# Feed forward of a two-layer diffusion step: gate and up products by a seven-product scheme, all products up before all products down

## The chip, the cores and the metric

The kernel runs on one core of a Trainium2 chip. The metric is the device time of one execution in microseconds (us), as the median of repeated runs.

## The reference

The model is a backbone of two layers on 1024 latent tokens and 128 context tokens, with 1024 features. Each layer has a token mixer (differential attention in layer 0, windowed attention with a sink in layer 1) and a dense SwiGLU feed forward with 2816 inner columns; RMSNorm stands before and behind both, and a modulation computed from a condition gives shift, scale and gate.

```python
def swiglu(h, w_gate, w_up, w_down):
    return (jax.nn.silu(h @ w_gate) * (h @ w_up)) @ w_down

# per layer, for context (p) and latent tokens (s):
hs = pre_norm_modulate(xs, norm_g[i, 2], ms[3], ms[4])
xs = post_norm_residual(xs, swiglu(hs, w_gate[i], w_up[i], w_down[i]), norm_g[i, 3], ms[5])
```

All of it is in float32. The kernel splits each operand of a large product into a high and a low half that TensorE reads as float32r, and sums three products: high by high, high by low, low by high.

## The kernel before

The 1152 tokens are nine blocks of 128: blocks 0 to 7 are latent, block 8 is the context. The stages follow each other: projections of layer 0, attention, output projection with its norms (class `OProj`), feed forward (class `Ffn`), the same for layer 1. Inside a stage the order of work on TensorE, VectorE, ScalarE and GpSimd is written out by hand (`tc.manual_schedule`): each engine runs its instructions in the order in which the program issues them. The DMA queue is SyncE's alone, and its order is planned by the compiler.

`OProj.step(i)` handles one block: the products of block i (`proj`, two halves), the norms of the block before (`norms`, parts 0 to 2), and the transposition of the block before that (`turn_h`), which leaves its high and low halves in `hT`, in three chunks of three blocks.

`Ffn` goes through the 22 blocks d of 128 inner columns. For each it loads 512 KB of the gate's, the up and the down weights, and splits them (`halves`, `wsplit`: a cast on ScalarE, L96, and a subtraction on VectorE, L97). For each chunk, `half` makes the gate's and the up products (L1327 to L1329: eight blocks kb of features, three products each, 384 columns wide), `swiglu` makes the activations of the block, and `down` multiplies those of the block d before with its down weights (L1353 to L1355, 512 columns) and VectorE adds the sum to `yacc` in SBUF (L1359). So up and down products alternate, and the sums over d are kept in SBUF. The sums of the last two d and the norms behind them follow as a written list of steps (`TAIL`), in layer 0 together with the first projections of layer 1.

Beside the feed forward, `mod_task` computes later parts of the modulation: VectorE accumulates rows of `w_mod` scaled by the condition (L226, L229), the accumulator is split (L96, L97), and four small matmuls (L243) sum over the partitions. It is a generator, and the feed forward takes one step of it per chunk: the split is one step, the matmuls are the next. Layer 0 has six such tasks beside its feed forward, layer 1 one.

PSUM has eight rooms of 512 columns: four `b`, two `t`, two `u`. Transpositions of blocks use `u`.

Of the kernel before, what the change touches and what calls it, by code (L numbers as in the profile page):

```python
# [33 lines left out]
SG = 4  # L34
EPS = 1e-6
LAM_INIT = 0.8 - 0.6 * math.exp(-0.3 * 0)
# [4 lines left out]
def hybrid_step(ctx: ExitStack, tc: tile.TileContext, x_prompt, x_sample, cache_diff_k, cache_diff_v,  # L41
# [14 lines left out]
    # per layer: the six parts of the modulation for both conds, with the norms' gains worked in  # L56
# [4 lines left out]
    # ------------------------------------------------------------------ constants  # L61
# [5 lines left out]
    # column cd of sel[:, cd] is one, the other zero: sums over the partitions into row cd  # L67
# [69 lines left out]
    def pre_norm(rs, xt, G, sh, xn, eng=pool):  # L137
        """xn = xt * rs * G + sh"""
# [3 lines left out]
    def post_norm(yv, rs, gg, xt, xo, t, eng=pool):  # L142
        """xo = xt + gg * yv * rs, the product in t"""
# [6 lines left out]
    def turn_hT(ps, tb, xn, hT):  # L150
        """block tb, transposed and split, into hT"""
        ch, o = tb // 3, (tb % 3) * P
        for half in range(2):
# [4 lines left out]
            hi = hT[0][ch][:, half * 4:half * 4 + 4, o:o + P]  # L158
            lo = hT[1][ch][:, half * 4:half * 4 + 4, o:o + P]
# [8 lines left out]
    class Mod:  # L168
        """parts of the modulation on all partitions, for the cond of the block at hand"""
# [11 lines left out]
    def alloc_hT(pool_, hT=None, chunks=range(3)):  # L181
        """rooms for the transposed input in chunks of three blocks, halves apart"""
        hT = hT or [{}, {}]
        for ch in chunks:
            for f in range(2):
                hT[f][ch] = pool_.tile([P, KB, 3 * P], F32R, name=f"h{'hl'[f]}{ch}")
        return hT
# [13 lines left out]
    def rows_out(l, j, n0, n, r, br, gr):  # L201
        """r: rows of silu(cond) @ w_mod; adds the bias, works in the norm's gain, and keeps them"""
# [11 lines left out]
    def mod_task(sb, ps, l, j, ring):  # L214
        """One of the six 1024-wide parts of the modulation of layer l, for both conds; a generator of steps."""
# [30 lines left out]

    def step(gen, n=1):
# [14 lines left out]
    # ------------------------------------------------------------------ start: conditioning, first modulation  # L262
    class Start:
        """the first modulation, and the first norm block by block"""
# [5 lines left out]
        def modulation(self, hooks):  # L270
            """hooks: by number of the piece of w_mod, what is loaded before it and what follows its split"""
# [45 lines left out]
            # the rows as columns, a feature a partition  # L317
# [19 lines left out]
        def spread(self, j):  # L337
            """the samples' columns as rows on all partitions: a column on all columns times the identity"""
# [35 lines left out]
        def modulate(self, tb):  # L374
            """the gain and the shift of each feature, and the split"""
            ch, o, cd, ts = tb // 3, (tb % 3) * P, cond_of(tb), []
# [10 lines left out]
            for half, t in enumerate(ts):  # L387
                hi, lo = [self.hT[f][ch][:, half * 4:half * 4 + 4, o:o + P] for f in range(2)]
# [11 lines left out]
    def small_params(sb):  # L400
        """lambda, the gain of the norm of the heads, the sinks"""
# [15 lines left out]
    class Ring:  # L417
        """rooms for weights as they come and for their two halves, 4 KiB each, taken in turn"""
# [15 lines left out]

    def ring_rooms(pool_, tags):
        """lays rooms out in the order of their tags"""
# [19 lines left out]
    class Qkv:  # L456
        """columns n * 512.. of the projection of block tb, in steps: products, rope and split, transposes"""

        def __init__(self, l, ps, sb, ring, hT):
            self.l, self.ps, self.sb, self.ring, self.hT = l, ps, sb, ring, hT  # L460
            self.cache = [x[0, 0].rearrange("t h d -> t (h d)") for x in
# [12 lines left out]
        def mm(self, n, tb, k0=0, k1=KB, mid=()):  # L474
            ch, o = tb // 3, (tb % 3) * P
# [3 lines left out]
            for kb in range(k0, k1):  # L479
# [4 lines left out]
                xh, xl = [self.hT[s][ch][:, kb, o:o + P] for s in range(2)]  # L484
# [5 lines left out]
        def split(self, key, x, g, dst, t0, eng=pool):  # L490
            """x[:, 64 g], split, for dst[:, :, t0:t0+128]"""
# [90 lines left out]
        def run(self, order, gens, hooks, g0=0):  # L582
            """hooks: by number of the step, what goes before the products and what goes after them"""
            seq = [(n, tb) for n in order for tb in range(NTB)]
            for i in range(len(seq) + 2):
# [12 lines left out]
                if i < len(seq):  # L598
                    k, tb = i // NTB, seq[i][1]
                    if k + 1 < len(order):  # L600
                        ws = self.ws.setdefault(order[k + 1], [])
                        for k2, (t0, t1) in enumerate(((5, 6), (6, 7), (7, 8), (7, 8))):
                            if tb == t0:
                                ws.append(Wqkv(self.l, self.ring, order[k + 1], k2))
                            if tb == t1:
                                ws[k2].split()
# [1064 lines left out]
```

## Time and profile before

| | |
|---|---|
| median of 3 runs | 3241.43 us |
| lowest and highest run | 3238.78 and 3243.96 us |
| span of the profiled execution, first to last instruction | 3245.7 us |
| instructions | 43729 |
| mean granted clock of TensorE | 0.988 of full speed |
| DMA traffic | 343.87 MB, mean 106 GB/s |

The profile is of one execution on the chip. PE is TensorE's matmuls, PEld its weight loads, DVE is VectorE, ACT ScalarE, POOL GpSimd, SP SyncE, whose queue issues the DMAs. The span of that execution is 4.3 us longer than the median of the runs; no time of its own is listed beside the span.

### The profile page before, as it was taken

What the parts mean: (1) busy time and instruction counts of PE and PEld (TensorE: products, weight loads), DVE (VectorE), ACT (ScalarE), POOL (GpSimd) and SP (SyncE); (2) the same over time, 40 slices, a digit from 0 to 9 for tenths busy, and PEclk for the clock granted to TensorE, in tenths of its full rate; (3) what the DMA queues carried; (4) which work ended last, traced back from release to release, by engine and by line L of the source; (5) the groups of instructions that cost most, each with busy time, mean ns of one, the idle gap of its engine ahead of it and who ended that gap; (6) DMA issues with size and microseconds to landing.
All of it is one profiled execution on the core that took longest, in us unless ns stands there. A gap on an engine that the chain in (4) does not pass through costs nothing. (4 is left out here: it accounts for less than half of the span.)

```text
span 3245.7 us, 43729 instructions
## 1 busy us (share of the span) xinstructions
PE 3107.3 (96%) x16942; PEld 2745.1 (85%) x16942; DVE 2125.8 (65%) x3138; ACT 1081.0 (33%) x2097; POOL 1006.9 (31%) x963
## 2 busy tenths in 40 slices
PE   8999989888999999999999799999999999999997
PEld 5888777777789999999999687777789999999997
DVE  6777388887556666766666944998566544444445
ACT  6332277776551111111112324776431111111112
POOL 2544299999330000000000644666220000000002
PEclk9999999999999999999999899999999999999999
DMA  6665633432442222222223454333442211111113
GB/s 216 205 214 185 204 94 118 130 118 69 140 137 87 76 72 74 82 67 72 85 66 107 163 167 135 111 112 106 138 145 66 65 39 40 46 46 46 39 40 117
DMA packets 309030, 343.87 MB, mean 106 GB/s; under 512 B 13124, under 2 KB 242540, under 8 KB 308696
## 3 DMA queue, kind: packets, MB, share of 16 engines
q1 hardware_dynamic: 308824, 341.09, 33.8%
q8 instruction: 134, 2.20, 0.3%
q14 instruction: 72, 0.59, 0.1%
HBM read 263.62 MB, written 77.41 MB: 105 GB/s over the span
## 5 line engine op out<-in xcount | busy, mean ns | idle before, releaser
L1327 PE MATMUL gu<-hh,fhi 128*128 128x384 f32 x2112 | 708.8, 336 | 0.1
L1328 PE MATMUL gu<-hl,fhi 128*128 128x384 f32 x2112 | 708.6, 336 | 0.2
L1329 PE MATMUL gu<-hh,flo 128*128 128x384 f32 x2112 | 708.2, 335 | 0.0
L1359 DVE TENSOR_TENSOR yacc<-dacc,yacc 128x512 f32<-128x512 f32 x720 | 476.4, 686 | 250.1 <-PE dacc L1355 243.2
L104 POOL TENSOR_SCALAR ah<-sg 128x384 fp32r<-128x384 f32 x132 | 72.3, 548 | 1535.0 <-DVE sg L1338 1535.0
L96 ACT CAST fhi<-fraw 128x1024 fp32r<-128x1024 f32 x132 | 138.6, 1052 | 854.4 <-PE gu L1328 384.7
L1327 PEld LDWEIGHTS gu<-hh,fhi 128*128 128x128 f32 x2112 | 396.4, 188 | 14.4 <-issue 0.8
L1328 PEld LDWEIGHTS gu<-hl,fhi 128*128 128x128 f32 x2112 | 396.4, 188 | 11.6 <-DVE hl L161 1.1
L1329 PEld LDWEIGHTS gu<-hh,flo 128*128 128x128 f32 x2112 | 396.4, 188 | 10.5 <-issue 0.3
L1355 PE MATMUL dacc<-fhi,al 128*128 128x512 f32 x792 | 312.3, 394 | 0.0
L1354 PE MATMUL dacc<-flo,ah 128*128 128x512 f32 x792 | 311.8, 394 | 0.0
L1353 PE MATMUL dacc<-fhi,ah 128*128 128x512 f32 x792 | 309.3, 391 | 2.4 <-DVE yacc L1359 1.7
L486 PE MATMUL qacc<-whi,hh 128*128 128x512 f32 x648 | 262.0, 404 | 0.6 <-ACT hh L389 0.4
L488 PE MATMUL qacc<-whi,hl 128*128 128x512 f32 x648 | 255.9, 395 | 4.3 <-DVE hl L161 4.3
L487 PE MATMUL qacc<-wlo,hh 128*128 128x512 f32 x648 | 255.3, 394 | 0.5 <-DVE wlo L100 0.5
L1338 DVE TENSOR_TENSOR sg<-gu,sg 128x384 f32<-128x384 f32 x132 | 73.4, 556 | 270.6 <-PE gu L1329 270.6
L714 POOL TENSOR_TENSOR aT<-a,aT 128x512 fp32r<-128x512 f32 x186 | 240.1, 1291 | 15.5
L229 DVE SCALAR_TENSOR_TENSOR macc<-wmod,sc,macc 128x512 f32<-128x512 f32 x280 | 212.5, 804 | 34.8 <-DMA wmod<-in_w_mod_dram 34.6
L674 DVE TENSOR_REDUCE nm<-S 128x1 f32<-128x1280 f32 x128 | 190.3, 1487 | 50.8 <-PE S L667 50.8
L1337 ACT ACTIVATE sg<-gu 128x384 f32<-128x384 f32 x132 | 64.3, 487 | 443.9 <-PE gu L1329 437.9
L97 DVE TENSOR_TENSOR flo<-fraw,fhi 128x1024 fp32r<-128x1024 f32 x132 | 161.7, 1225 | 76.9 <-ACT fhi L96 76.7
L667 PE MATMUL S<-K,q 128*128 128x512 f32 (+1 forms) x768 | 184.3, 377 | 12.1 <-ACT e L679 7.9
(265 smaller groups left out, 5944.5 us busy)
## 6 DMA issues: line engine op xcount, KB each, us to landing
wmod<-in_w_mod_dram SPq DMA_DIRECT2D x80, 512.0 KB
fraw<-in_w_gate_dram SPq DMA_DIRECT2D x44, 512.0 KB
fraw<-in_w_up_dram SPq DMA_DIRECT2D x44, 512.0 KB
fraw<-in_w_down_dram SPq DMA_DIRECT2D x44, 512.0 KB
qT_d<-xT SPq DMA_DIRECT2D x36, 512.0 KB
q<-qT_d SPq DMA_DIRECT2D x64, 256.0 KB
wraw<-in_w_qkv_diff_dram SPq DMA_DIRECT2D x24, 512.0 KB
kT_d<-xT SPq DMA_DIRECT2D x22, 512.0 KB
```

Of the source, the lines that this page charges most:

```text
L229: dve.scalar_tensor_tensor(out=acc[cd], in0=w[:, a, :], scalar=sc[:, kb, cd:cd + 1], in1=acc[cd], op0=ALU.mult, op1=ALU.add)
L486: pe.matmul(acc, lhsT=xh, rhs=hi[:, a, :], start=(kb == 0), stop=False)
L487: pe.matmul(acc, lhsT=xh, rhs=lo[:, a, :], start=False, stop=False)
L488: pe.matmul(acc, lhsT=xl, rhs=hi[:, a, :], start=False, stop=(kb == KB - 1))
L714: (dve if self.last else pool).tensor_tensor(out=lo, in0=x, in1=hi.bitcast(F32), op=ALU.subtract)
L1327: pe.matmul(g, lhsT=hi[:, kb, :], rhs=xh[:, kb, :], start=(kb == 0), stop=False)
L1328: pe.matmul(g, lhsT=hi[:, kb, :], rhs=xl[:, kb, :], start=False, stop=False)
L1329: pe.matmul(g, lhsT=lo[:, kb, :], rhs=xh[:, kb, :], start=False, stop=(kb == KB - 1))
L1353: pe.matmul(acc, lhsT=ah[:, o:o + P], rhs=hi[:, cs], start=(i == 0), stop=False)
L1354: pe.matmul(acc, lhsT=ah[:, o:o + P], rhs=lo[:, cs], start=False, stop=False)
L1355: pe.matmul(acc, lhsT=al[:, o:o + P], rhs=hi[:, cs], start=False, stop=(i == len(parts) - 1))
L1359: dve.tensor_tensor(out=y[:, cs], in0=acc, in1=y[:, cs], op=ALU.add)
```

## The change

The weights of a block d are taken as a matrix of two by two: rows gate (1) and up (2), columns the first and the second half of the 1024 features. The input is two by two as well: its halves of features, and two halves of tokens. Blocks are paired for this, (0, 4), (1, 5), (2, 6), (3, 7), and block 8 is cut in two; the first two pairs are column group (part) 0 with 256 columns, the rest is part 1 with 320. Seven products of sums of these blocks replace the eight block products (a scheme of Strassen's kind): sums of weights are made on GpSimd for each d, sums of inputs once a layer, each split into halves. Products to be added to each other stay in one PSUM sum.

All products up come first, and the activations go to a DRAM tensor `a_d`. Then all products down follow, in three groups of three blocks; for each group and d the down weights and the activations are loaded, split and multiplied, and the sum over d stays in PSUM. The modulation's task is a new one, `mod_task_lean`. The order of the blocks changes in the output projection and behind.

```diff
+OORDER = (0, 1, 4, 5, 2, 6, 3, 7, 8)
+GROUPS = ((0, 1, 4), (5, 2, 3), (6, 7, 8))
+DORDER = sum(GROUPS, ())
...
+    def mod_task_lean(ps, l, j, mroom, rooms):
...
+                while len(ws) < min(kb + 2, KB):
+                    ws.append(new(mroom[1:][len(ws) % 2], [P, 512], F32, "wmod"))
...
+                yield kb == KB - 1
+            pre = rows_in(iter([junk[0:2, i * 512:(i + 1) * 512] for i in range(2)]), l, j, half * 512, 512)
+            hi, lo = [rooms.take((P, D), F32R, "mhl") for _ in range(2)]
+            act.copy(out=hi, in_=macc)
+            dve.tensor_tensor(out=lo, in0=macc, in1=hi.bitcast(F32), op=ALU.subtract)
+            r = ps.tile([2, 512], F32, name="mrow", tag="u", bufs=2)
+            for cd in range(2):
+                for i, x in enumerate((hi, lo)):
+                    pe.matmul(r, lhsT=sel[:, cd, :], rhs=x[:, cd * 512:(cd + 1) * 512], start=(cd + i == 0),
+                              stop=(cd + i == 2))
+            rooms.give(hi, lo)
+            rows_out(l, j, half * 512, 512, r, *pre)
+            yield False
...
+    class Halves:
...
+        def first(self, part, c, a, raw):
+
+            for i, name in enumerate(("B11", "B21")):
+                act.copy(out=self.hi[name, part][:, :, c:c + a[i].shape[-1]], in_=a[i])
+                dve.tensor_copy(out=raw[:, i], in_=a[i])
...
+            dve.tensor_tensor(out=T1, in0=b[0], in1=B11, op=ALU.subtract)
+            act.copy(out=B22, in_=b[1])
+            dve.tensor_tensor(out=T, in0=B22, in1=b[0], op=ALU.subtract)
...
+            low(dve, "B11", B11)
+            low(dve, "T3", T)
...
+        def pair(self, part, c, xs, rooms):
+
+            raws, n = [], P if len(xs) == 2 else P // 2
+            for i, x in enumerate(xs):
+                tps = self.turned(x)
...
+        def prep(self, d, what):
...
+            if what == "s0":
+                s = w[d, "r", "s0"] = rooms.take(name="fsum")
+                pool.tensor_tensor(out=s[:, 0:512], in0=A21, in1=A22, op=ALU.add)
+                pool.tensor_tensor(out=s[:, 512:D], in0=s[:, 0:512], in1=A11, op=ALU.subtract)
...
+        PRODUCTS = (("X", 0, 0, "B11"), ("Z", 0, 1, "B21"), ("X", "s0", 1, "T2"), ("Y", "s1", 0, "T3"),
+                    ("X", "s0", 0, "T1"), ("X", "s1", 1, "B22"), ("Y", 1, 1, "T4"))
...
+        PREP = (("s0",), ("s1", "hg"), ("lg", "ha"), ("la", "hb"), ("lb",), ("u",), ())
...
+            for kb in range(4):
+                pe.matmul(o, lhsT=hi[:, kb, :], rhs=xh[:, kb, :], start=(first and kb == 0), stop=False, **more)
+                pe.matmul(o, lhsT=hi[:, kb, :], rhs=xl[:, kb, :], start=False, stop=False, **more)
+                pe.matmul(o, lhsT=lo[:, kb, :], rhs=xh[:, kb, :], start=False, stop=(kb == 3),
+                          **more)
+            self.sums(d, k, part)
...
+            elif k == 4:
+                t["4"] = self.post("U4", part)
+                act.copy(out=t["4"], in_=X)
+                dve.tensor_tensor(out=t["4"], in0=Y, in1=t["4"], op=ALU.add)
...
+            for d in range(NDF):
+                if d == 0:
+
+                    for k in range(7):
+                        self.product(0, k, 0)
+                        for f in late[k] if k < len(late) else ():
+                            f()
+                    for k in range(7):
+                        self.product(0, k, 1)
+                        self.free(0, k)
+                        self.ahead(1, k)
+                elif d < NDF - 1:
+                    for k in range(7):
+                        for part in range(2):
+                            self.product(d, k, part)
+                        self.free(d, k)
+                        self.ahead(d + 1, k)
+                        if not hold or len(self.rooms.free) >= 2:
+                            hold = next(gen, False)
+                else:
+                    assert next(gen, None) is None
+                    for part in range(2):
+                        for k in range(7):
+                            self.product(d, k, part)
...
+        def ahead(self, d, k):
+            for what in self.PREP[k]:
+                self.prep(d, what)
+            if k == 6 and d + 1 < NDF:
+                self.fetch(d + 1)
...
+            self.lead, self.nlast = 2 + l, 3 + l
...
+        def load_w(self, g, d):
+
+            rooms, c, n = self.rooms, g * 3 * P, 3 * P
+            x, a = rooms.take(name="fraw"), rooms.take(name="araw")
+            dma(out=x, in_=w_down[self.l, d * P:(d + 1) * P, :])
+            dma(out=a[:, 0:n], in_=a_d[d * P:(d + 1) * P, c:c + n])
...
+            for i, (g, d) in enumerate(steps):
+                if i + self.lead < len(steps):
+                    self.load_w(*steps[i + self.lead])
+                if g < 2 or d < NDF - self.nlast:
+                    for j in range(3):
+                        self.down(g, d, j)
...
                 for i in range(-2, NTB - 1):
                     op.step(i, hooks)
+                tags = ["w2", "r1", "w3", "w0", "w1", "b0", "b1", "b2"]
+                f.begin(Rooms([where[tag] for tag in tags]))
+                f.fetch(0)
+                op.step(NTB - 1, hooks)
+                op.norms(TB_PROMPT, 0)
+                for what in ("s0", "s1", "hg"):
+                    f.prep(0, what)
+                op.norms(TB_PROMPT, 1)
+                op.norms(TB_PROMPT, 2)
+                for what in ("lg", "ha", "la", "hb", "lb", "u"):
+                    f.prep(0, what)
...
+                late = [[lambda: self.pair(1, 0, 2, 6), lambda: f.fetch(1)], (), [lambda: self.pair(1, P, 3, 7)], (),
+                        [lambda: self.pair(1, 2 * P, TB_PROMPT)]]
...
+            hooks = {i: (steps(a), steps(b)) for i, (a, b) in enumerate((
+                ("", "00 01 02 10"), ("", "11 12 20"), ("", "21 22 30"), ("", "31 32"), ("t0", "t1"), ("t2", "")))}
```

In `prep` the names h and l stand for the high and the low half of the first gate weight (g) and of the two sums (a, b), and u for both halves of the last block. The last lines are the steps that follow the products of the first projections of layer 1.

## Rows read from the trace of the kernel before

**Rows 1.** The page, busy time of the engines over the span.
```profile
PE 3107.3 (96%) x16942; PEld 2745.1 (85%) x16942; DVE 2125.8 (65%) x3138; ACT 1081.0 (33%) x2097; POOL 1006.9 (31%) x963
```
**Rows 2.** Windows, feed forward of layer 0: length, busy times, clock, DMA share, GB/s.
```profile
956.10:1773.60 817.50, 816.78 (x4314) 761.01 (x4313) 535.17 (x808) 121.73 (x174) 39.37 (x67) 1.00 0.26 78
```
**Rows 3.** The page, costliest groups: busy us, mean ns of one, idle before.
```profile
L1327 PE MATMUL gu<-hh,fhi 128*128 128x384 f32 x2112 | 708.8, 336 | 0.1
...
L1327 PEld LDWEIGHTS gu<-hh,fhi 128*128 128x128 f32 x2112 | 396.4, 188 | 14.4 <-issue 0.8
```
**Rows 4.** Timeline, TensorE in the feed forward: start and duration in us.
```profile
1501.42 0.39 PE L1353 MATMUL dacc<-fhi,ah 128*128 128x512 f32 x1
...
1503.51 0.33 PE L1327 MATMUL gu<-hh,fhi 128*128 128x384 f32 x1
...
1765.22 0.33 PE L1327 MATMUL gu<-hh,fhi 128*128 128x384 f32 x1
...
1773.57 0.39 PE L1353 MATMUL dacc<-fhi,ah 128*128 128x512 f32 x1
...
1790.61 0.39 PE L1353 MATMUL dacc<-fhi,ah 128*128 128x512 f32 x1
```
**Rows 5.** Timeline, TensorE in the attention of layer 0.
```profile
606.57 0.28 PE L724 MATMUL av<-aT,V 128*128 128x256 f32 x1
...
607.41 0.29 PE L725 MATMUL av<-aT,V 128*128 128x256 f32 x1
```
**Rows 6.** Groups by line and shape, whole span.
```profile
L97 DVE TENSOR_TENSOR flo<-fraw,fhi 128x1024 fp32r<-128x1024 f32 x132 | 161.7, 1225 | 76.9 <-ACT fhi L96 76.7
...
L161 DVE TENSOR_TENSOR hl<-tp_n,hh 128x512 fp32r<-128x512 f32 x66 | 42.5, 683 | 24.2 <-ACT hh L160 23.7
...
L96 ACT CAST fhi<-fraw 128x1024 fp32r<-128x1024 f32 x132 | 138.6, 1052 | 854.4 <-PE gu L1328 384.7 <-PE dacc L1355 293.6 <-issue 83.8
...
L1337 ACT ACTIVATE sg<-gu 128x384 f32<-128x384 f32 x132 | 64.3, 487 | 443.9 <-PE gu L1329 437.9 <-DVE macc L226 5.8
...
L714 POOL TENSOR_TENSOR aT<-a,aT 128x512 fp32r<-128x512 f32 x124 | 162.1, 1307 | 10.3
...
L229 DVE SCALAR_TENSOR_TENSOR macc<-wmod,sc,macc 128x512 f32<-128x512 f32 x280 | 212.5, 804 | 34.8 <-DMA wmod<-in_w_mod_dram 34.6
...
L243 PE MATMUL mrow<-mhi,sel 128*2 128x512 f32 x40 | 15.8, 394 | 0.0
```
**Rows 7.** The same view, two groups of norms on VectorE.
```profile
L147 DVE SCALAR_TENSOR_TENSOR yacc<-yacc,rs,bc 128x1024 f32<-128x1024 f32 x17 | 34.6, 2034 | 0.6
...
L139 DVE SCALAR_TENSOR_TENSOR xn<-K,rs,bc 128x1024 f32<-128x1024 f32 x9 | 11.6, 1284 | 0.7
```
**Rows 8.** Timelines, one load of w_mod: its issue, and VectorE's wait.
```profile
1104.13 0.37 SPq L221 DMA_DIRECT2D wmod<-in_w_mod_dram  x1
...
1107.97 1.41 DVE L229 SCALAR_TENSOR_TENSOR macc<-wmod,sc,macc 128x512 f32<-128x512 f32 x2 [3.87 <-DMA wmod<-in_w_mod_dram]
```
**Rows 9.** Timelines, first up product of layer 0, and VectorE in block 8's norm.
```profile
956.14 0.34 PE L1327 MATMUL gu<-hh,fhi 128*128 128x384 f32 x1
...
962.32 1.41 DVE L147 SCALAR_TENSOR_TENSOR xn<-oacc,rs,q 128x512 f32<-128x512 f32 x2
...
970.67 1.23 DVE L140 TENSOR_TENSOR xn<-xn,bc 128x1024 f32<-128x1024 f32 x1
```
**Rows 10.** Windows, from layer 0 to layer 1.
```profile
1760.00:1900.00 140.00, 123.62 (x592) 103.08 (x590) 103.85 (x149) 48.74 (x94) 69.14 (x49) 0.93 0.50 166
...
1780.00:1800.00 20.00, 19.06 (x88) 15.52 (x87) 17.93 (x22) 10.73 (x23) 9.60 (x4) 1.00 0.65 229
...
1800.00:1820.00 20.00, 13.47 (x52) 10.25 (x51) 18.95 (x21) 8.36 (x18) 16.60 (x6) 0.77 0.50 165
```
**Rows 11.** L1353 over the span (min/median/max ns, first and last start), and VectorE's end.
```profile
L1353 PE MATMUL dacc<-fhi,ah x792: 387/389/500, 975.2 to 3229.2; 128*128 128x512 f32 x198
...
3241.34 0.69 DVE L148 TENSOR_TENSOR xt<-yacc,xt 128x512 f32<-128x512 f32 x1
```

More of the change, by code (lines that the diff above doesn't have):

```diff
@@ L179, in get, with alloc_hT @@
             return self.t
[L181 to L187, printed above, removed]
+    def alloc_hT(rooms):
+        return [[new(rooms[2 * pos + f], [P, KB, P], F32R, "h" + "hl"[f]) for pos in range(NTB)] for f in range(2)]
     def rows_in(tiles, l, j, n0, n):
@@ L387, in modulate @@
             for half, t in enumerate(ts):
-                hi, lo = [self.hT[f][ch][:, half * 4:half * 4 + 4, o:o + P] for f in range(2)]
+                hi, lo = [self.hT[f][tb][:, half * 4:half * 4 + 4, :] for f in range(2)]
                 act.copy(out=hi, in_=t)
@@ L433, in w, with new, __init__, take @@
             return self.take(1, shape, dt, name)
+    def new(room, shape=(P, D), dt=F32, name="room"):
+        pool_, tag, bufs = room
+        return pool_.tile(list(shape), dt, name=name, tag=tag, bufs=bufs)
+    class Rooms:
+        def __init__(self, rooms, lent=()):
+            self.free, self.lent, self.of = list(rooms), set(lent), {}
+        def take(self, shape=(P, D), dt=F32, name="room"):
+            room = self.free.pop(0)
+            t = new(room, shape, dt, name)
+            self.of[id(t)] = (t, room)
+            return t
+        def give(self, *ts):
+            for t in ts:
+                room = self.of.pop(id(t))[1]
+                if room not in self.lent:
+                    self.free.append(room)
     def ring_rooms(pool_, tags):
@@ L582, in run @@
         def run(self, order, gens, hooks, g0=0):
-            seq = [(n, tb) for n in order for tb in range(NTB)]
+            seq = [(n, tb) for n in order for tb in self.order]
             for i in range(len(seq) + 2):
@@ L1504, in begin @@
[L1504 to L1512 removed]
+            where = dict(zip(("x0", "x1", "x2", "x3"), H[14:]))
@@ new lines, in begin, with pair @@
+            where.update(zip(("x4", "w0", "w1", "w2", "w3", "r1", "b0", "b1", "b2"), L))
+            self.temps = L[8 + l:]
+            def pair(part, c, *tbs):
+                rooms = [where[f"x{OORDER.index(tb) % 5}"] for tb in tbs]
+                f.hv.pair(part, c, [op.xn[tb] for tb in tbs], [*rooms, *self.temps][:3])
+                if part:
+                    f.rooms.free += rooms
+            self.pair = pair
+            for k, c, tbs in (((5, 0), 0, (0, 4)), ((6, 0), P, (1, 5))):
+                hooks.setdefault(k, []).append(lambda c=c, tbs=tbs: pair(0, c, *tbs))
@@ L1514, in begin, with room @@
+            hooks[5, 0].insert(0, lambda: f.hv.lay(0, iter(H)))
+            def room(tag, shape, dt, name):
+                return new(where[tag], shape, dt, name)
             with tc.manual_schedule(engines=ENGINES):
-                op.begin(self.ps, self.wo_tiles, hT,
-                         lambda tag, shape, dt, name: ra.tile(shape, dt, name=name, tag=tag, bufs=1),
-                         ("r2", "w6", "w7")[0:2 + l])
-                for i in range(-2, NTB - 2):
+                op.begin(self.ps, self.wo_tiles, None, room, ("b0", "b1", "b2")[0:2 + l])
+                for i in range(-2, NTB - 1):
@@ new lines, in down @@
+        def down(self, stack, ahead=lambda ring: ()):
+            l, f, H = self.l, self.f, self.H
+            R = ring_rooms(stack.enter_context(sbuf(f"D{l}", "right")), [f"d{i}" for i in range(18)])
+            yx, cut = R[0:6], R[6:16] if l == 0 else R[6:8]
+            mods = [H[12:15], H[15:18]] if l == 0 else [cut[0:1], cut[1:2]]
+            hT = alloc_hT(H) if l == 0 else None
+            rest = [r for r in R[6:] if r not in cut]
+            self.ring = Ring(cut[0:2], cut[2:] + rest + yx)
+            f.rooms.free += [r for r in self.old.free if r not in H] + rest
+            with tc.manual_schedule(engines=ENGINES):
+                f.downs(mods, yx, hT, ahead(self.ring))
+            self.low.close()
@@ L1524, in hybrid_step @@
         gemm_psum(ps)
-        hT = alloc_hT(hp)
+        hT = alloc_hT(ring_rooms(hp, [f"h{i}" for i in range(2 * NTB)]))
         ring = Ring([(wq, "raw", 4)], [(wq, "w", 12)])
@@ L1617, in hybrid_step @@
     before1.close()
-    f = la.f
-    with sbuf("Y", "right") as Y, la.early:
-        f.main(Y, [(1, 5)])
-        f.tail()
+    la.ffn([(1, 5)])
+    la.down(ctx)
 _INS = ['x_prompt', 'x_sample', 'cache_diff_k', 'cache_diff_v', 'cache_swa_k', 'cache_swa_v', 'c', 'c_ctx',
```

561 lines of the change are left out of this document (322 added, 239 removed).

## The prediction

> **What bounds the kernel now.** I read the page first, for the bound, then the windows, then single instructions. TensorE is busy 96% of the span [rows 1]. In the feed-forward stretch of layer 0 it is busy 816.8 of 817.5 us at the full granted clock, while VectorE is at 65%, ScalarE at 15% and GpSimd at 5% [rows 2]: only TensorE's own work counts there, and 720 sums of yacc on VectorE cost nothing. What one matmul costs cannot be read from its duration: L1327 shows 336 ns, its weight load 188 ns [rows 3], but the timeline shows them overlapping. From 1765.22 to 1773.57 there are 48 starts of 384 columns, 0.174 us each; from there to 1790.61 75 starts of 512 columns, 0.227 us each; mixed with up products the nine from 1501.42 to 1503.51 took 0.232 us each [rows 4]. I sum starts, not durations.
>
> **Up products.** Before: 22 blocks d, 3 chunks, 2 weights, 8 kb, 3 halves, so 3168 matmuls a layer. Now each d has 7 products of 4 kb and 3 halves on two column groups: 84 matmuls of 256 and 84 of 320 columns. Seven eighths of the columns, but 3696 instructions a layer, each with its own weight load. What does a narrow one cost? Attention has 256-wide ones with weight loads of their own: the seven from 606.57 to 607.41 took 0.120 us each [rows 5], and others there slightly less; I take 0.119. The load hides at that width. For 320, between 0.119 and 0.174, I take 0.146. One d: 84 x (0.119 + 0.146) = 22.3 us, against 144 x 0.174 = 25.1. Over 44 d **-122 us**; with 0.120 and 0.150 it is -105, with 0.117 and 0.144 -138.
>
> The Trainium skill ("Perfetto Trace Analysis", opening note) says that matmul busy time misjudges the distance to the limit because matmuls are pipelined; here the durations (336 ns for 384, 0.28 us for 256 columns, some 0.31 for 320) would give 49.6 us a d against 48.4, no gain. The rows on starts agree with the page.
>
> **What surrounds them in the steady state.** Per d: VectorE splits three weights at 1.23 us and a half one at 0.7, and adds out of PSUM six times at about 0.45 (0.683 for 512 columns): 7.1 us. ScalarE casts at 1.05 us three times, half once, and moves ten sums at no more than 0.49: 8.7 us. GpSimd makes four 512-wide sums at 1.31 and four narrower products: 8.4 us [rows 6]. Each fits under 22.3 us of TensorE; cost 0. If an engine needs more, the difference is paid for every d.
>
> **The modulation.** The old task gave up its turn between splitting the accumulator and the selection matmuls, so these found their operands: L243 shows no idle before it [rows 6]. The new one issues cast, subtraction and matmuls in one step, and TensorE, in order, stands at them with the next products behind. The cast waits behind ScalarE's own sums of that product (0.5 us, and in some positions a 1.05 us weight cast), then 1.05, then 1.23 on VectorE. By the place among the seven products, k, this makes 1.8 us (k = 1, 6), 3.0 (0, 4), 3.5 (5), 4.4 (2), and k = 3 is passed over for want of two free rooms; mean 2.9. Seven tasks of two halves: 14 x 2.9 = **+41 us** (bounds 14 x 1.8 = 25 and 14 x 4.5 = 63). No such wait exists before, so these are chains of rows, not rows.
>
> In the same stretch VectorE carries 14 accumulations of 0.75-0.80 us and two first ones per half: with split and bias 14 us, and 9.1 us of the above in nine steps k, so 23 us against TensorE's 32 with its wait. It is tight, because 128x1024 operations from SBUF that take 1.28 us alone average 2.03 us beside GpSimd's additions [rows 7], and because w_mod now has two rooms only; a wait of 3.87 us for it, with 3.84 us from issue to use, is in the trace already [rows 8]. GpSimd is active a third of the time, so I add 3 us of stretching and 3 us of waits: 29 us, still under 32. Cost 0 beyond the wait above.
>
> **The opening of each feed forward.** Before, the first up products start right behind the last projection matmul, at 956.14, since chunk 0 was ready; block 8's norm runs behind them from 962.32 to 971.90, 9.6 us [rows 9]. Now the low half of the first gate weight is issued on VectorE behind the whole norm of block 8. The sums of squares, one cast and the square root come first (2.7 us after the projection; in the trace 6.2, with block 7 in the way), then 9.6 us, then 1.2: TensorE waits 13.5 us (bounds 10.8, without the lead, and 17, with the old one). The second product waits 1.6 us for the half u, fourth in that queue. Then three pairs of blocks are turned between the products of column group 0 through two PSUM rooms, shared with Z: second block and next Z each wait for two or three VectorE operations of 0.69 us behind the previous pair's eight. That is some 7 us a layer. After such idleness the clock falls to its 1.2 GHz level for a while: in the window 1800-1820, with 6.5 us idle, the granted clock is 0.77 [rows 10]; I put 2 us on that. Sum 23 us a layer net of a gap of 0.7 before, **+46 us** (bounds 24, little more than the first wait, and 70, with 17 for it and the pairs at twice their price).
>
> **Products without cover.** In the first and last d the column groups go one after the other, so the fifth product waits for a copy of X out of PSUM and its latency, 0.8 us: six times besides the opening, **+5 us**.
>
> **Down products.** 2376 matmuls of 512 columns, as before. Undisturbed by up products they may run at 0.227 for 0.232: **-6 us** (bounds -12 and 0). Each step of 18 matmuls, 4.2 us, brings 512 KB of weights (now three times a layer) and 192 KB of activations: 170 GB/s, and the trace has 229 in 1780-1800 [rows 10]. Loads are issued two steps ahead (8.4 us; three in layer 1): 3.8 us landing [rows 8], 0.8 for the second, 1.05 + 1.23 + 0.55 for the split, so 7.4. It fits; for hiccups and the first step **+6 us** (0 to 30). The stores of a_d, 0.6 MB a d, run beside products and are read 22 d later; nothing.
>
> **Tails.** From 1760 to 1900 TensorE idles 16.4 us of 140 and the clock is 0.93 [rows 10]: nine blocks' norms follow the last sums, with VectorE busy up to 19 of 20 us. Now six blocks are finished and turned during the down steps, and three are normed beside the first projections of layer 1. Two turns stand before projection 4 though block 7's last norm part is issued just ahead, some 7 us on VectorE and GpSimd. **-10 us** (-18 to 0). At the end the last L1353 starts at 3229.2, so products end near 3230, and the last addition ends at 3242.0 [rows 11]: 15.5 us from products to the end of the span, 3.7 of them for the last store. Now the sum stays in PSUM: squares 1.6, root and reciprocal 1.0, four operations of 0.75, the same 3.7 for the store, 9.4: **-6 us**.
>
> **Sum.** -122 + 41 + 46 + 5 - 6 + 6 - 10 - 6 = -46 us on a span of 3245.7. The profiled execution is 4.3 us (0.13%) above the median of the runs, 3241.4; the difference scales by less than 0.1 us, so I forecast **3196 us**. A change of 0.2%, 6.5 us, is about what can be told from none.
>
> **Rivals.**
> *VectorE falls behind in layer 0* (the other side). For: operations stretched to twice their length and waits for w_mod. Against: 6 us of room in 32. If all its SBUF work were stretched as in [rows 7], 19 us become 30, with 4 for PSUM and 5 for loads 39 us per half, 7 over, x 12 = 84 us: 3280 us. It decides from 36 us per half, 4 over, where 12 x 4 eats the 46. The Trainium skill ("GPSIMD Engine Reference", 1. Specifications) says that GpSimd shares its SBUF interfaces with VectorE and contends with instructions that have two SBUF inputs, as all of these do; the trace agrees, 2.03 against 1.28 us.
> *The losses at their upper bounds* without that: opening 70, modulation 63: 3241 - 122 + 63 + 70 + 5 - 6 + 6 - 16 = 3241 us, no change.
> *The losses at their lower bounds*: 24 + 25, down -12, tails -24, opening hiccup 0: 3241 - 122 + 49 + 5 - 36 = 3137 us. For: the engines' order may give slack where I let every wait end last.
> *The down steps starve.* Before, each weight was loaded once, far ahead. Landing at 7 us instead of 3.8 makes 10.6 for two steps, 1.1 a step too much over the 66 steps of layer 0, +73: 3269 us; from 6.2 us on it eats the gain. Against: rooms are reused one to two steps early, so issues may come sooner.
> *The weight load sets the pace of narrow matmuls* (the step does nothing): each at 188 ns would make 168 x 0.188 = 31.6 us a d, +286: 3604 us. Rows 5 speak against it.
>
> **Chances.** Forecast as worked out: 0.63. Lower bounds: 0.10. Upper bounds, about even: 0.12, of which 0.05 still counts as faster. VectorE 0.09, starving 0.05, weight loads 0.01. So faster 0.78, same 0.07, slower 0.15. The range leaves out the lower half of the second case and the three slow ones: 3146 to 3246; the forecast's own range is 3155 to 3228.
>
> **What would show it.** Right: spacing of the new up matmuls 0.119 and 0.146, a d of layer 1 at 22-23 us and of layer 0 about 26; 13 us of idle TensorE behind the last projection of either layer, released by VectorE's subtraction; 14 waits of 2-4 us at the selection matmuls; down steps at 4.1-4.2 us with no wait for a load. Wrong: TensorE waiting in layer 0 for sums or splits outside those 14 places (VectorE), for down weights (loads), a wider spacing than 0.27 for the pair of widths, or an opening that hides behind something I took to be later in the queues.

## Result and the profile after

The changed kernel takes **3378.84 us** (median; 3375.96 to 3381.83) against 3242.69 us of the kernel before: ratio 1.0422, 95% interval 1.0407 to 1.0437, 136 us slower. Forecast were 3196 us, range 3146 to 3246. It went to the side of the rival "the down steps starve", and 110 us beyond the time that this rival gave.

The page of the changed kernel, engines over the span of 3378.7 us, and the chain that ended last, by engine:

```profile
PE 3078.1 (91%) x17998; PEld 2663.0 (79%) x17998; DVE 2011.9 (60%) x2749; ACT 1423.9 (42%) x2764; POOL 1404.4 (42%) x1226
...
PE 47%; DVE 9%; DMA 7%; ACT 5%; POOL 3%; issue 2%; ACTq 0%; SPq 0%; DVEq 0%; POOLq 0%
```

TensorE is busy 29 us less than in [rows 1], but its share fell from 96% to 91% of a longer span. So the products may well be cheaper, and the question is where TensorE's 300 us without work stand; the 7% of the chain (the shares follow back from the last instruction) that are transfers, 0% before, are a first hint. Windows say more (length, busy us and instructions of PE, PEld, DVE, ACT, POOL, then granted clock, DMA share, GB/s): opening, up and down steps of layer 0, then the same three of layer 1.

```profile
core 0: us, PE busy (x) PEld busy (x) DVE busy (x) ACT busy (x) POOL busy (x), PEclk, DMA share, GB/s
970.00:985.00 15.00, 2.47 (x11) 2.27 (x12) 10.39 (x11) 4.43 (x7) 5.44 (x3) 0.64 0.30 105
...
1040.00:1120.00 80.00, 73.70 (x523) 71.78 (x522) 60.43 (x73) 24.98 (x47) 30.37 (x24) 0.96 0.41 122
...
1600.00:1640.00 40.00, 33.22 (x125) 22.74 (x125) 10.92 (x13) 10.32 (x14) 0.00 (x0) 1.00 0.38 127
...
2565.00:2575.00 10.00, 7.75 (x33) 6.95 (x34) 7.21 (x9) 5.18 (x9) 1.29 (x1) 0.50 0.18 54
...
2720.00:2800.00 80.00, 80.00 (x604) 80.00 (x603) 26.20 (x36) 26.28 (x51) 26.68 (x27) 1.00 0.22 67
...
3200.00:3240.00 40.00, 40.00 (x177) 32.80 (x176) 28.88 (x28) 15.98 (x25) 9.78 (x3) 1.00 0.77 266
```

In layer 0's opening TensorE works 2.5 us of 15, and in layer 1's, behind its first wait, at half its clock. Past that, layer 1 is what was forecast of both layers: 604 up products in 80 us, 0.1325 us on average, so 0.265 for a pair of 256 and 320 columns (forecast 0.119 + 0.146), and 177 down products in 40 us (175 of them start there). Layer 0 gets 125 down products into the same 40 us, at full clock and with *less* traffic, 127 GB/s against 266. That is no shortage of bandwidth.

The projection of layer 0 ends 12.7 us later (last matmul 968.55 against 955.90). From there to the end of layer 1's projection, before from 955.90 to 2397.0, now to 2550.1, it takes 1581.5 us instead of 1441.1 (+140); the rest shrinks from 848.7 to 828.6 (-20). So layer 1 gained, and what was lost was lost in layer 0. What TensorE waited for (us in total, times, longest), in layer 0's down steps and, below, behind the projection of layer 1:

```profile
PE dacc L1613 <- ACT ahl L1599: 37.8, 39, 3.2
PE dacc L1614 <- DVE fl L1598: 15.0, 39, 2.2
PE dacc L1613 <- ACT yacc L1621: 14.1, 2, 7.2
...
PE guX L1502 <- DVE fl L1473: 12.8, 1, 12.8
PE guX L1500 <- ACT U L1525: 5.7, 2, 4.0
```

The first three lines, 67 us, are less than the stage lost: a matmul is shown for 0.39 us although the next one can start 0.227 us behind it [rows 4], which hides a part of each wait. One load, followed on three engines (start, duration, and in brackets what the engine waited for), shows what stands behind the first of these:

```profile
1615.78 1.23 DVE L1598 TENSOR_TENSOR fl<-fraw,fh 128x1024 fp32r<-128x1024 f32 x1 [4.20 <-ACT fh L1597]
...
1617.04 0.33 SPq L1594 DMA_DIRECT2D fraw<-in_w_down_dram  x1
...
1620.71 1.05 ACT L1597 CAST fh<-fraw 128x1024 fp32r<-128x1024 f32 x1 [4.54 <-DMA fraw<-in_w_down_dram]
...
1621.79 1.23 DVE L1598 TENSOR_TENSOR fl<-fraw,fh 128x1024 fp32r<-128x1024 f32 x1 [4.31 <-ACT fh L1597]
```

The subtraction of one weight ends at 1617.01; SP issues the next load at 1617.04; its cast starts 3.67 us later; the next subtraction starts 6.01 us after the last one. One load is under way at a time, and a step of 4.12 us of matmuls takes a whole load chain. The code says why. A load takes five rooms from a list in the order in which they came free (raw weight, raw activation, three for the splits) and gives the two raw ones back at once. Layer 0 has 11 lasting rooms there, since those of H go over to hT and the modulation rows. Two steps loaded ahead hold six; of the five left, the oldest is always the raw room of the load just before, which is free only when VectorE has subtracted from it.

### The profile page after: what moved, and what is told of

The parts are those of the page before. It is cut to its first block, busy times and chain, and to the rows that moved or that the text cites. A ratio compares the mean times of both kernels' runs of the same rounds, so it can differ in the third digit from the quotient of the medians.

```text
span 3378.7 us, 47921 instructions
## 1 busy us (share of the span) xinstructions
PE 3078.1 (91%) x17998; PEld 2663.0 (79%) x17998; DVE 2011.9 (60%) x2749; ACT 1423.9 (42%) x2764; POOL 1404.4 (42%) x1226
## 4 chain that ended last, share of the span: by engine, by line
PE 47%; DVE 9%; DMA 7%; ACT 5%; POOL 3%; issue 2%; ACTq 0%; SPq 0%; DVEq 0%; POOLq 0%
DMA fraw<-in_w_down_dram 7%; PE guX L1500 6%; PE guX L1502 6%; PE guX L1501 6%; PE dacc L1613 3%; PE dacc L1614 3%; PE dacc L1615 3%; PE guY L1500 3%; PE guY L1502 3%; PE guY L1501 3%; DVE fl L1598 2%; ACT fh L1597 2%; PE guZ L1500 1%; PE guZ L1502 1%; PE guZ L1501 1%
## 5 line engine op out<-in xcount | busy, mean ns | idle before, releaser
L1613 PE MATMUL dacc<-fh,ahl 128*128 128x512 f32 x792 | 322.4, 407 | 53.9 <-ACT ahl L1599 37.8
L1614 PE MATMUL dacc<-fl,ahl 128*128 128x512 f32 x792 | 321.2, 406 | 15.1 <-DVE fl L1598 15.0
L1598 DVE TENSOR_TENSOR fl<-fraw,fh 128x1024 fp32r<-128x1024 f32 x132 | 164.5, 1247 | 272.9 <-ACT fh L1597 269.8
L1615 PE MATMUL dacc<-fh,ahl 128*128 128x512 f32 x792 | 321.3, 406 | 0.0
L1597 ACT CAST fh<-fraw 128x1024 fp32r<-128x1024 f32 x132 | 138.1, 1047 | 268.8 <-DMA fraw<-in_w_down_dram 262.7
L1613 PEld LDWEIGHTS dacc<-fh,ahl 128*128 128x128 f32 x792 | 152.6, 193 | 103.2 <-ACT ahl L1599 55.5
L1614 PEld LDWEIGHTS dacc<-fl,ahl 128*128 128x128 f32 x792 | 152.7, 193 | 60.5 <-DVE fl L1598 28.0
L1615 PEld LDWEIGHTS dacc<-fh,ahl 128*128 128x128 f32 x792 | 152.3, 192 | 46.0 <-DVE ahl L1600 12.7
L735 ACT ACTIVATE e<-S,nm 128x1280 f32<-128x1280 f32 x128 | 171.4, 1339 | 7.2 <-DVE nm L730 7.1
L723 PEld LDWEIGHTS S<-K,q 128*128 128x128 f32 x768 | 137.4, 192 | 44.1 <-ACT e L735 19.3
L110 POOL TENSOR_SCALAR aT<-a 128x512 fp32r<-128x512 f32 x192 | 154.0, 802 | 23.8 <-ACT a L759 23.8
L1473 DVE TENSOR_TENSOR fl<-fsum,fh 128x1024 fp32r<-128x1024 f32 x88 | 107.2, 1219 | 95.1 <-ACT fh L1471 94.8
```

Source lines behind the costliest of these rows:

```text
L723: pe.matmul(S[:, j:j + n], lhsT=self.q[:, f, m, i * P:(i + 1) * P], rhs=kv[self.h][0][:, m, j:j + n], start=(f == 0), stop=(f == 1))
L1598: dve.tensor_tensor(out=lo, in0=x, in1=h.bitcast(F32), op=ALU.subtract)
L1613: pe.matmul(acc, lhsT=ah, rhs=hi[:, cs], start=(d == 0), stop=False)
L1614: pe.matmul(acc, lhsT=ah, rhs=lo[:, cs], start=False, stop=False)
L1615: pe.matmul(acc, lhsT=al, rhs=hi[:, cs], start=False, stop=(d == NDF - 1))
```

## The experiments

Except in 4 and 9, each edit is made to the changed kernel, 3378.8 us.

**1. Lead 1 in layer 0.**

```diff
-            self.lead, self.nlast = 2 + l, 3 + l
+            self.lead, self.nlast = 1 + 2 * l, 3 + l
```


> One edit: layer 0 loads its down weights one step ahead instead of two. Theory 1 (rooms): with lead 2 and 11 rooms the raw weight room passes straight from one load to the next, so a step takes a whole load chain, landing 3.7 + cast 1.05 + subtraction 1.23 = 5.9-6.0 us; with lead 1, three rooms fewer are held and a load can start while the one before is still being split. Steps return to 4.1-4.3 us, the down stage of layer 0 from 397 to 275-290 us, the time to 3258-3275 us. Theory 2 (the transfer itself: three reads of the weights plus a_d are too much for the queues, each landing late): a shorter lead gives less cover, so the stage stays at 397 us or gets longer, time 3375 us or more.

Measured: **3281.5 us** (1.0117 of before, 1.0104 to 1.0131), -97, a little less than theory 1 said. Loading *less* far ahead made the steps faster: only three rooms are held then, and the oldest of the eight left came free two steps ago. Windows, then waits of the down steps:

```profile
1600.00:1640.00 40.00, 40.00 (x177) 32.83 (x176) 16.89 (x20) 13.48 (x19) 0.00 (x0) 1.00 0.57 181
...
1800.00:1840.00 40.00, 38.18 (x176) 30.62 (x175) 28.19 (x30) 19.04 (x30) 7.19 (x3) 1.00 0.70 236
```
```profile
PE dacc L1614 <- DVE fl L1598: 3.3, 5, 0.9
PE dacc L1615 <- DVE ahl L1600: 2.6, 4, 0.8
PE dacc L1613 <- ACT ahl L1599: 1.9, 1, 1.9
```

The stage, from first to last start of L1613, shrank from 396.7 (1563.7 to 1960.4) to 292.8 us (1570.7 to 1863.5), a little above what was expected, and it began 7 us later. The transfer as the cause is out: it now brings 181 GB/s.

**2. The same shortage given to layer 1**, which has no turns and no query weights beside its down steps: lead 2 and 11 rooms.

```diff
-            self.lead, self.nlast = 2 + l, 3 + l
+            self.lead, self.nlast = 2, 3
...
-                    self.old, f.rooms = f.rooms, Rooms(H[0:12], () if l else H)
+                    self.old, f.rooms = f.rooms, Rooms(H[0:12], H)
...
-            f.rooms.free += [r for r in self.old.free if r not in H] + rest
+            f.rooms.free += [r for r in self.old.free if r not in H] + rest[:2]
```


> The changed kernel with layer 1's down steps given what layer 0's have: 11 rooms and lead 2, the rooms of H lent and not returned, eight of the further rooms left out. Theory 1 (the count of rooms alone starves the steps, 5.9 us each instead of 4.12): layer 1's down stage grows from 272 to 380-395 us, the time to 3485-3500 us. Theory 2 (layer 0's steps starve because of what runs beside them there: query weights, norms, turns, stores): 3400 us or less.

Measured: **3493.8 us**, +115. Window and waits in layer 1's down steps:

```profile
3200.00:3240.00 40.00, 31.80 (x120) 24.21 (x119) 13.68 (x17) 13.88 (x21) 0.00 (x0) 0.87 0.38 123
```
```profile
PE dacc L1613 <- ACT ahl L1599: 42.7, 47, 4.4
```

The stage went from 278.5 to 391.8 us: 11 rooms at lead 2 do it, with no turns and no query weights beside them.

**3. The selection matmuls one product behind the split.** The split is now passed over at products 2 and 3, and no longer whenever fewer than two rooms are free.

```diff
             dve.tensor_tensor(out=lo, in0=macc, in1=hi.bitcast(F32), op=ALU.subtract)
+            yield False
             r = ps.tile([2, 512], F32, name="mrow", tag="u", bufs=2)
...
-                        if not hold or len(self.rooms.free) >= 2:
+                        if not hold or k not in (2, 3):
```


> One edit: the modulation task yields once more between the subtraction of its accumulator and the selection matmuls, so that one product lies between. Theory 1: the 14 waits of 3.3 us at the selection matmuls go and nothing takes their place: -40 to -50 us, 3329-3340 us. Theory 2 (VectorE is the bound of the up stage of layer 0, the wait is only where it shows): the waits move to the sums and the up stage stays as it is, 3365 us or more.

Measured: **3328.6 us** (1.0265, 1.0251 to 1.0279), -50. In the changed kernel TensorE waited 28 times at the 56 selection matmuls, 42.7 us in all:

```profile
PE mrow L273 <- ACT mhl L268: 23.9, 14, 2.5
PE mrow L273 <- DVE mhl L269: 18.8, 14, 2.0
```

Next, layer 0 from the second d to the last but one, of the changed kernel and then of this one, with the same count of matmuls:

```profile
1029.60:1544.00 514.40, 478.04 (x3410) 463.75 (x3409) 343.07 (x424) 157.53 (x292) 193.66 (x160) 0.96 0.38 113
```
```profile
1030.70:1505.70 475.00, 463.23 (x3410) 453.93 (x3409) 350.59 (x424) 158.27 (x292) 192.55 (x160) 0.99 0.42 122
```

The stretch is 39.4 us shorter, although its waits fell only from 36.4 to 11.8 us. The rest goes with the granted clock, 0.99 for 0.96: an estimate from these two rows is 3% of some 500 us, 15 us. Nothing took the place of the waits, so VectorE was not the bound.

**4. Both together.**

> Both edits of the first two experiments together: lead 1 in layer 0's down steps, and the selection matmuls one product behind the split. They lie in different stages. Theory 1 (two independent losses): the gains add, 3378.8 - 97.5 - 50 = 3231 us (3226-3237), under the kernel before. Theory 2 (the later weights of the first down steps or VectorE tie them together): 3245 us or more.

Measured: **3229.3 us** (0.9955, 0.9939 to 0.9972): they add, and this is 0.45% faster than the kernel before. TensorE's waits from 1020 to 1530 now:

```profile
PE mrow L274 <- DVE s L1519: 6.5, 5, 3.2
PE guX L1501 <- ACT U L1526: 4.5, 2, 4.0
PE mrow L274 <- DVE mhl L269: 3.0, 7, 0.4
```

**5. The opening: first splits ahead of block 8's norm** (layer 0, which has a spare room for it).

```diff
...
                 for what in ("s0", "s1", "hg"):
                     f.prep(0, what)
+                if l == 0:
+                    f.prep(0, "lg")
+                    f.rooms.free.insert(0, f.rooms.free.pop())
+                    f.prep(0, "u")
                 op.norms(TB_PROMPT, 1)
                 op.norms(TB_PROMPT, 2)
-                for what in ("lg", "ha", "la", "hb", "lb", "u"):
+                for what in ("lg", "ha", "la", "hb", "lb", "u") if l else ("ha", "la", "hb", "lb"):
```


> One edit: in layer 0 the split of the first gate weight and of half the up weight is issued ahead of block 8's two norm parts instead of behind them. Theory 1 (the first wait stands in the middle of a chain that VectorE's queue bounds: the other splits and the three pairs still follow the norm): the wait of 11.9 us at the first low half falls under 4 us, but later ones grow; 3 to 7 us saved, 3372-3376 us. Theory 2 (the first wait is paid in full): 10 us or more, 3369 us or less. Theory 3: nothing, 3379 us.

Measured: **3378.5 us**, nothing. Waits of TensorE from 940 to 1045:

```profile
PE tp_n L1374 <- DVE raw L1382: 10.7, 3, 9.0
...
PE guX L1502 <- DVE fl L1473: 1.1, 1, 1.1
```

The wait of 11.9 us at the first low half fell to 1.1, and one of 9.0 came up at the next pair's transposes, whose copies stand behind the same norm in VectorE's queue. So that queue bounds this part of the opening, and this wait had no price of its own.

**6. TensorE kept at work during that wait**, with 80 matmuls without use.

```diff
+            if (d, k, part) == (0, 0, 0):
+                z = self.ps.tile([P, 512], F32, name="warm", tag="u", bufs=2)
+                for _ in range(20):
+                    for kb in range(4):
+                        pe.matmul(z[:, 0:n], lhsT=hi[:, kb, :], rhs=xh[:, kb, :], start=(kb == 0), stop=(kb == 3))
```


> One edit: 80 matmuls of 256 columns without use (the first gate weight's high half against B11's, into a PSUM room of Z not yet begun) ahead of the first product of each layer, some 9.6 us, inside the wait of 12-13 us for the first low half. Theory 1 (behind the first wait TensorE runs at its 1.2 GHz level, granted clock 0.50-0.67 in 2550-2585, and this costs time of its own): the clock of the opening rises to 0.9 or more, 6 to 16 us saved in the two layers, 3363-3373 us. Theory 2 (VectorE's chain bounds the opening, at either clock): the clock rises but the time stays within 3 us of 3379. Theory 3 (the dummies run into the products): 3382 us or more.

Measured: **3373.3 us**, -5.5, at the upper end of theory 1, though the clock did not reach the 0.9 expected there. The window of layer 1 where the pairs are turned, of the changed kernel and then of this one:

```profile
2565.00:2585.00 20.00, 15.46 (x72) 14.18 (x72) 14.70 (x18) 10.31 (x18) 6.24 (x4) 0.59 0.22 67
```
```profile
2565.00:2585.00 20.00, 14.66 (x80) 13.17 (x80) 16.30 (x20) 11.15 (x20) 9.65 (x7) 0.74 0.22 66
```

After the 13 us without work TensorE ran mostly at its 1.2 GHz level (0.59 on average); with work in the wait it was granted 0.74 there. The filling is worth some 3 us a layer. That it is not more would fit a stretch that VectorE bounds at either clock, as in 5; how much a full clock would give was not measured.

**7. All subtractions of the pairs on VectorE.** First only those of the two pairs beside each projection (`dve` for `pool` in four places, where part is 0), then those of the opening too.

> One edit: the four subtractions that each pair turned during the projection gives to GpSimd go to VectorE. Theory 1 (the projection of layer 0 ends 12.7 us later than before because GpSimd gets to its scaling of the attention output late, 14.2 us of waits against 3.6): 7 to 12 us saved, 3367-3372 us. Theory 2 (VectorE's longer queue costs as much, or the delay is from the transposes): within 4 us of 3379.

> One edit: the four subtractions of every pair that GpSimd makes go to VectorE, those of the feed forward's opening too. Theory 1 (VectorE's 128x512 subtractions take 1.4-1.8 us beside GpSimd's and 0.68 alone, so twelve alone, 8.2 us, are shorter than the eight beside them, 9.3, and GpSimd is free for the sums of the next weights, which ScalarE stands waiting for): 8 to 15 us saved, 3364-3371 us. Theory 2 (VectorE is the longest queue of the opening and gets four more operations a pair): 3385-3400 us.

Measured: **3376.5** and **3373.6 us**: the first is inside its theory 2, so GpSimd's share is not what delays the projection; the second gives 5 us where 8 to 15 were expected. VectorE in the first pair of layer 1's opening, with one of GpSimd's operations beside it, changed kernel, then with all on VectorE:

```profile
2575.99 0.68 DVE L1395 TENSOR_TENSOR B21l<-raw,B21h 128x512 fp32r<-128x512 f32 x1
2576.59 1.76 DVE L1395 TENSOR_TENSOR T2l<-raw,T2h 128x512 fp32r<-128x512 f32 x1
2578.28 1.76 DVE L1395 TENSOR_TENSOR T1l<-raw,T1h 128x512 fp32r<-128x512 f32 x1
...
2577.76 1.72 POOL L1395 TENSOR_TENSOR B22l<-raw,B22h 128x512 fp32r<-128x512 f32 x1
```
```profile
2575.03 0.68 DVE L1395 TENSOR_TENSOR T1l<-raw,T1h 128x512 fp32r<-128x512 f32 x1
2575.63 0.68 DVE L1395 TENSOR_TENSOR B22l<-raw,B22h 128x512 fp32r<-128x512 f32 x1
2576.23 0.68 DVE L1395 TENSOR_TENSOR T4l<-raw,T4h 128x512 fp32r<-128x512 f32 x1
```

An operation of 0.68 us takes up to 1.76 beside GpSimd's, and GpSimd needs 1.3 to 1.7 us for one itself, so four more on VectorE cost it nothing in time. The Trainium skill ("GPSIMD Engine Reference", 1. Specifications) says that GpSimd shares its SBUF interfaces with VectorE and contends with instructions of two SBUF inputs; these rows agree.

**8. The projection of layer 0.** TensorE waits 14.2 us there at the transposes of the attention output for GpSimd's scaling of it (L1267), 3.6 before. Scaling ahead of the pairs; then, as a probe of whose queue the pairs lengthen, the low halves of the two pairs subtracted twice on VectorE, or their high halves cast twice on ScalarE.

```diff
...
-*(((None, 0), (2, "scale")), ((None, 0), (2, "scale")))[self.l]
+*(((2, "scale"), (None, 0)), ((None, 0), (2, "scale")))[self.l]
...
```


> One edit: in each step of layer 0's projection the scaling of the next attention output is issued ahead of the pair that is turned there, instead of behind it. Theory 1 (the 14.2 us of waits at the transposes of the attention output, 3.6 before, come from the scaling's square root and reciprocal queued behind the pair's casts and subtractions on ScalarE and VectorE, then on GpSimd): the waits fall to 4-6 us and 6 to 11 us are saved, 3368-3373 us. Theory 2 (the engines' total work is the bound there, as when GpSimd's part of the pairs was moved and 2 us came of it): within 3 us of 3379.

> The changed kernel, in which VectorE makes each of its five subtractions to low halves twice in the two pairs beside layer 0's projection: 10 more operations of 0.68 us alone, up to 1.75 beside GpSimd, 7 to 14 us in all. Theory 1 (VectorE's queue carries the projection's chain of norms, so the pairs' 8 operations each are the 12.7 us): 6 us or more above 3378.8. Theory 2 (VectorE has slack there): within 3 us.

> The changed kernel, in which ScalarE makes each of its five casts to high halves twice in the same two pairs: 10 more of 0.62 us, 6.2 us in all. Theory 1 (VectorE's queue, not ScalarE's, is the chain): at most 3 us above 3378.8. Theory 2 (ScalarE, which takes the sums of squares and square roots of the norms, is the chain or both in turn): 4 to 8 us above.

Measured: **3379.0**, **3385.1** (3383.0 to 3387.5) and **3379.9 us**. With the scaling first, from 820 to 970:

```profile
PE tp_n L1374 <- DVE raw L1382: 8.4, 2, 5.5
PE guX L1500 <- ACT fh L1471: 3.7, 1, 3.7
...
PE tp_o L1298 <- POOL V L1267: 0.9, 1, 0.9
```

The wait moved, as in 5. Ten more subtractions on VectorE cost 6.2 us, and the wait for L1267 grew to 21.9; ten more casts on ScalarE 1.0, inside the spread. So VectorE's queue carries this stretch too, and the pairs' operations on it, with GpSimd beside them, are the likeliest cause of the delay. That all 12.7 us are theirs was not tried by leaving the pairs out.

**9. Everything together** (the edits of 1, 3, 6 and the second of 7), with one more edit of the opening: the second d's sums s0 and s1 on GpSimd right behind the second pair. In the changed kernel ScalarE casts such a sum as soon as GpSimd has made it, and its copy of X, for which TensorE waits, stands behind that cast (layer 1):

```profile
2605.72 1.04 ACT L1471 CAST fh<-fsum 128x1024 fp32r<-128x1024 f32 x1 [2.41 <-POOL fsum L1460]
...
2606.67 0.42 ACT L1525 COPY U<-guX 128x320 f32<-128x320 f32 x1
```

```diff
...
-[lambda: self.pair(1, P, 3, 7)]
+[lambda: self.pair(1, P, 3, 7), lambda: f.prep(1, "s0"), lambda: f.prep(1, "s1")]
...
```


> Five edits together: lead 1, selection one product behind the split, the 80 filling matmuls, the pairs' subtractions on VectorE, and one new: the sums s0 and s1 of the second d are issued behind the second pair instead of behind the last product of column group 0, since GpSimd was idle for 35 us there while ScalarE then stood at a cast of that sum and a copy of X behind it (4.0 us in each layer). Theory 1 (they act on different waits): 3229.3 - 5.5 - 5.2 - 4 to 8 = 3210-3215 us. Theory 2 (all opening edits shorten the same chain on VectorE, so they don't add): 3219-3226 us.

Measured: **3211.2 us** (0.9909, 0.9895 to 0.9923). As theory 1 said; if the gains add, 3229.3 - 5.5 - 5.2 leaves 7.4 us for the new edit, which was not run alone.

Then, in place of lead 1, lead 2 with ten rooms that lie idle until layer 1's query weights come, and lead 1 only behind that:

```diff
...
+            self.rooms.free += self.cut
...
+                if self.cut and (g, d) == (2, 1):
+                    self.lead = 1
+                    self.rooms.lent |= set(self.cut)
+                    self.rooms.free = [r for r in self.rooms.free if r not in self.cut]
...
```


> The same, but instead of lead 1 throughout: layer 0's down steps use ten rooms that lie idle until the query weights of layer 1 need them, at lead 2; from the second step of the last group on they are left, at lead 1. Theory 1 (what lead 1 still loses, 293 us against 273, is the depth of the loads: casts issued only one step ahead behind the norms): 6 to 14 us less than the combination with lead 1, 3198-3208 us. Theory 2 (it is VectorE and ScalarE, busy with norms and turns in those groups): within 3 us of that combination.

Measured: **3205.5 us** (0.9880, 0.9867 to 0.9894), 1.2% under the kernel before; the down stage went from 296.1 to 289.1 us. The gain of 5.7 us is a little less than expected. So layer 0's down steps run at lead 2 as well as at lead 1, once they have the rooms. With the scaling first as well:

> The version with more rooms, and the scaling of the attention output issued ahead of the pairs in layer 0's projection. Alone this order took the waits at the output's transposes from 14.2 to 0.9 us, and nothing of the time. Theory 1 (what took the gain back was the pairs' own slow chain and block 8's norm behind it, which have since become shorter): 4 to 9 us less than 3205.5, 3196-3201 us. Theory 2 (VectorE and ScalarE together bound the projection with the pairs in it, whatever the order): within 3 us of 3205.5.

Measured: **3205.2 us**, so no gain here either.

## Why the prediction was wrong

By its own terms, forecast against measured:

- **Up products, -122: right.** 168 x 0.1325 = 22.3 us a d, as forecast; start to start, a d of layer 1 without modulation takes 22.35.
- **Down feed, +6: this step failed.** "Loads are issued two steps ahead (8.4 us; three in layer 1) ... It fits". The load is *called* two steps ahead, but is issued only when a room is free, and in layer 0 that is one chain of landing, cast and subtraction (3.67 + 1.05 + 1.23) before its use. The stage took 396.7 us; 66 x 18 products at layer 1's 0.2286 (40 us / 175) make 271.6, and 24 up products that run inside the stage 3.5. That is +122; layer 1's stage, 278.5 us, is +3 by the same count. Lead 1 gave 97 back, more rooms 6 more. I had counted time ahead and not rooms. The rival that named starving had a chance of 0.05 and asked for a landing of 7 us; it was 3.7, and what it held against itself, the reuse of rooms, was the cause.
- **Openings, +46, and products without cover, +5: undersized.** From the last projection matmul to the first product of the second d are 61.0 us (968.55 to 1029.6) and 63.1 (2550.1 to 2613.2); without the 22.3 of a d, 79.5 for both layers against 51. The first wait was right (11.9 and 12.8 for 13.5). Missed were a wait of 4.0 us in each layer, in which a copy of X on ScalarE stands behind a cast that waits for GpSimd's late sums (I put such copies at 0.8). On the low clock I had put 2 us a layer; filling the first wait gave some 2.8 back in each. Three edits together gave 18 us.
- **Modulation, +41: the waits right, the price undersized.** The waits add up to 42.7 us. But the twenty d from the second on take 514.4 us in layer 0 and 458.9 (2613.2 to 3072.1) in layer 1, and 20 x 22.35 are 447: 79 us too many, of which 56 selection matmuls at 0.23, which the kernel before has too, make 13. So the new task costs 66 us. The sum had no term for TensorE's clock behind these waits, which by the estimate of experiment 3 is most of the rest. Splitting the step gave 50 back. No VectorE bound, as forecast.
- **Projection, 0: left out.** It ends 12.7 us later in layer 0; the pairs turned beside it lengthen VectorE's queue, which is the likeliest cause (experiment 8).
- **Tails, -10 and -6: right.** From the last down product of layer 0 (1799.1 before, 1960.9 now) to the last projection matmul of layer 1 it takes 589.1 us instead of 597.6, -9; at the end 8.0 us from the start of the last down product (3370.7) instead of 16.1 (3229.6), -8.

The measured profile lies 179 us above the forecast span of 3199.7. Down feed makes 119 of it, openings 28, modulation 25, projection 13, and the tails take 1 off. These are 5 us too many, which I can't assign. What the turns of six blocks between the down steps cost was not separated from the feed. With the rooms, the order of the modulation and the opening mended, the kernel comes to 3205 us. That this lies inside the range given does not bear the forecast out, which was for the kernel without these edits.

## What to carry to other kernels

How far ahead a load is written says little by itself; count the rooms that are held when it is issued, and ask which instruction frees the one it takes. With a list that hands out the oldest free room, fewer steps ahead can keep more loads under way. Where many operations of one engine's queue stand between two stages, moving one wait may only show the next: price the queue, not the wait. And a short wait of TensorE can cost more than it lasts, where the clock falls behind it as here: compare the whole stretch, not the sum of the waits.

## What was not expected of the hardware

- Products of 256 and 320 columns follow each other at 0.1325 us although their weight loads last 0.188 us each: in the 80 us from 2720 to 2800 the 603 loads add up to 113 us, so loads, as the profile shows them, overlap one another as well as the matmuls.
- Behind a wait of 13 us TensorE's granted clock was 0.50, its 1.2 GHz level, for ten more microseconds, in which it was busy 7.75 (2565 to 2575); 80 matmuls without use in that wait, in each layer, made the kernel 5.5 us faster.
- Behind short waits the clock fell too. Around the first two waits at the selection matmuls, 2.5 and 0.9 us, the granted clock was 0.75 from 1060 to 1066; with the split of experiment 3 it was 1.00 there.
